# Pinned splits and earlier loads of late operands, tile 19 by token halves, and a shorter sum for one product in a hybrid attention and MLP trunk

## The chip, the core and the metric

The kernel runs on one core of a Trainium2 chip. A core has a matrix engine (PE), three engines for elementwise work (DVE, ACT, POOL), a queue that issues transfers (SP; POOL issues some too) and 16 DMA engines that carry them. Every engine works through its own queue in order, and semaphores hold an instruction back until what it reads or overwrites is ready. Matrix products are accumulated in PSUM, eight banks of 128x512 numbers; all else on the core lies in SBUF.

The metric is the device time of one execution in microseconds (us). The kernel before took a median of 1145.42 us in three runs (1144.83 to 1148.57).

## The reference

One layer of a streaming encoder with 1024 tokens and a model width of 1024, all in 32-bit floats:

```python
hn = rmsnorm(h, norm_mix_g);  z = hn @ w_in              # 1024 -> 512 pooling + 3 x 512 attention
a  = pool_mixer(u);  o = chunk_attention(q, k, v, rel_bias)
h  = h + concat([a, o]) @ w_out
hn = rmsnorm(h, norm_ffn_g);  up = hn @ w_up             # 1024 -> 2 x 2816
gt, val = up[..., :2816], up[..., 2816:]
gt = causal_dwconv(gt, conv_w, conv_b)                   # width 3 over tokens
h  = h + (gelu(gt) * val) @ w_down                       # 2816 -> 1024
hn = rmsnorm(h, norm_ple_g);  gate = sigmoid(hn @ w_ple_gate + b_ple_gate)
h  = h + gate * (p @ w_ple)
out = rmsnorm(h, final_g)
```

The change lies in the gated MLP (`w_up`, the convolution, `w_down`) and in the operands of the last stage (`w_ple`, `p`).

## The kernel before

**Numbers in two parts.** PE takes a rounded form of a 32-bit float, so each operand is cut into a rounded part and a remainder. `split` does that with two instructions: ACT copies the source into the rounded part (L133), then DVE subtracts that from the source (L134). A product is three matmuls (`mm3`, L128 to L130): high by high, high by low, low by high.

**Stages.** Attention and pooling mixer with the input projection run to about 275 us, the output projection to about 380 us, the MLP from there to about 998 us, and the projection of `p`, the gate and the final norm to the end.

**The up-projection.** The 2816 hidden features are 22 tiles (`NF`) of 128, numbered from 0. For each tile, the weights form a 2x2 block matrix (gate and value rows by two halves of the width) and the activations another (two halves of the width by two halves of the tokens, `HS`). A form of fast matrix multiplication takes seven products in place of eight; they carry the numbers 1 to 7, and `FORMS` says which weight blocks each one sums. A product is four `mm3` into one PSUM bank, 12 matmuls. `steps` holds the order of a tile's products: (1, 5, 6, 2, 7, 3, 4), except for tiles 0 and 1, parts of which are done ahead (`ahead`). For tile 1 the order is (5, 6, 2, 7, 3, 4). Below, (21, 6) is product 6 of tile 21.

For each product `prepare` loads the weight blocks it still needs from `w_up` into one of six raw buffers (`rawu`, SP, L695), sums them in place on DVE (`summed`, L699) and splits the sum into one of three weight buffers (`wu`). It does that three products ahead, and `fetch` asks for loads three further products ahead.

`step` then runs the product and moves its result on. `keep` copies a bank to SBUF on ACT (L784), `seed` copies one bank into another with a sign (L788), and the DVE lines 807 to 821 finish gate and value. A product that adds into a bank whose earlier content is still to be copied away has to wait for that copy. `gate` does the convolution and GELU: ACT (L833), DVE twice (L834, L835), ACT (L836). For tiles in `halved` it runs by token halves, otherwise once over 1024 tokens.

**The down-projection.** Tiles 0 to 19 go to `w_down` in five groups (0 to 4) of four tiles, by the same kind of fast multiplication: seven products per group in `DOWN_ORDER` (1, 2, 5, 4, 6, 7, 3), each of 24 matmuls into banks 4 to 7 (`down_next`). Their places between the up products are fixed (`places`, `downs`). A finished tile is written to device memory (`Yd`, SP, L891); `ask` loads blocks of it and of `w_down` into eight raw buffers (`RW`): one pair "one" and one pair "grow" for each side, weights `w` and activations `a`. The first block of a sum is a plain load by SP (L942), each further block is a load by POOL that adds to what is there (L940). `DOWN_W` and `DOWN_A` list the blocks. On the activation side product 4 sums four blocks, so each of its two buffers takes one plain load and three adding ones; product 6 adds one more block to product 5's sum in "grow". `split_next` splits the four buffers into `BQ` and `R`: w, w, a, a, with L133 and L134, or with L972 and L973 where the activation's sign is turned (products 2, 4, 7). Each split of a product waits until the product before has read the pair, so it falls between two down products. Below, (4,4) in "down (4,4)" is product 4 of group 4.

Tiles 20 and 21 are kept on the core (`store`, buffers `gv2`) and multiplied directly later (`down_mm`).

**Late operands.** The raw weights of tiles 20 and 21 (`w_down`), `w_ple` and `p` are loaded through `late_pair` into `rawu` buffers that have come free (SP, L1041) and split into `wd2`, `wp` and `pt`: twelve pieces of 256 KB. Six are written after products 2 and 3 of tile 21, six after that tile.

**What sets the order.** PE runs its instructions in the order of the program. For the other engines and for SP a planner chooses when the program is built: among the instructions that it takes to be ready at a moment of its own timetable it takes the one that stands first in the program, and those under `tc.high_priority(AHEAD)` are treated as if they stood 60 instructions earlier. So an instruction can come long before its place in the program. In the queue that results the order is then fixed, and an instruction whose data comes later than the timetable had it holds up all behind it.

## Time and profile before

| what | value |
|---|---|
| median of three runs | 1145.42 us |
| profiled execution, its own time | 1146.88 us |
| its span, first to last instruction | 1145.1 us |
| mean granted clock of PE | 0.995 |
| PE busy | 1129.9 us, 99%, 5675 matmuls |
| DVE busy | 888.2 us, 78% |
| ACT busy | 604.7 us, 53% |
| POOL busy | 146.8 us, 13% |
| moved by DMA | 125.89 MB, 110 GB/s |

A page of the profile gives for each engine its busy time, then the span in 40 slices, then the chain of waits and the costliest groups of instructions. A timeline row holds start, duration, engine, line, operation, tiles, shape, how many instructions it stands for, and in brackets how long the engine had been idle before it and what ended that. A row of stretches holds, for one stretch of the span, its length, the busy time of each engine with its number of instructions, the granted clock of PE, the share of the DMA engines in use and GB/s.

### The profile page before, as it was taken

Reading aid. Unit: us, or ns where it says so; the run is one execution under the profiler, and the core shown is the slowest. Engines: PE = TensorE matmul, PEld = TensorE weight load, DVE = VectorE, ACT = ScalarE, POOL = GpSimd, SP = SyncE. Lnnn points to the kernel's source line nnn. Section 1 sums busy time; section 2 is a strip of 40 time slices with the busy share of each in tenths; the row PEclk is TensorE's granted clock in tenths of the full one; section 3 lists DMA queues with packets and bytes.
Section 4 is the critical chain, followed back from the end, with each engine's and each line's share of the span. In section 5 each row is a group of like instructions: output and inputs, shape, how many; then the busy total and the mean of one; then the engine's idle time right before and its main releaser. Section 6 shows DMA issues by size and latency. Waiting matters only on the chain.

```text
span 1145.1 us, 15750 instructions
## 1 busy us (share of the span) xinstructions
PE 1129.9 (99%) x5675; PEld 958.2 (84%) x5675; DVE 888.2 (78%) x1541; ACT 604.7 (53%) x1068; POOL 146.8 (13%) x192
## 2 busy tenths in 40 slices
PE   9999999999999999999999999999999999999997
PEld 7988998888888778888888888888888887788897
DVE  7678878879658787888787878777887788986864
ACT  8568677765554554444444444443444344664644
POOL 0000000073002200120112011201120113000000
PEclk9999999999999999999999999999999999999999
DMA  7110101104500343575557655755575559320012
GB/s 265 37 49 31 50 12 68 40 28 151 172 19 10 97 128 117 140 172 140 144 144 162 158 148 146 173 141 145 152 172 138 145 148 183 114 92 19 1 74 74
DMA packets 65022, 125.89 MB, mean 110 GB/s; under 512 B 7344, under 2 KB 8624, under 8 KB 64944
## 3 DMA queue, kind: packets, MB, share of 16 engines
q1 hardware_dynamic: 50400, 98.60, 25.9%
q0 software_dynamic: 14400, 26.22, 14.1%
q8 instruction: 44, 0.72, 0.3%
q14 instruction: 34, 0.28, 0.1%
q10 hardware_dynamic: 144, 0.07, 0.0%
HBM read 110.18 MB, written 14.68 MB: 109 GB/s over the span
## 4 chain that ended last, share of the span: by engine, by line
PE 93%; issue 2%; ACT 2%; DMA 1%; DVE 1%; SPq 0%; POOL 0%; POOLq 0%; DVEq 0%; ACTq 0%
PE PS L128 28%; PE PS L129 28%; PE PS L130 28%; PE PS L367 2%; PE PS L385 1%; PE PS L384 1%; DMA F<-in_w_down 1%; PE PS L342 1%; PE PS L341 1%; DMA F<-in_w_qk 0%; PE PS L350 0%; PE PS L349 0%; PE PS L617 0%; DMA RW<-in_w_down 0%; ACT F L353 0%
## 5 line engine op out<-in xcount | busy, mean ns | idle before, releaser
L128 PE MATMUL PS<-R 128*128 128x512 f32 (+1 forms) x1176 | 443.2, 377 | 2.8 <-ACT F L784 2.1
L130 PE MATMUL PS<-R 128*128 128x512 f32 (+1 forms) x1176 | 438.4, 373 | 0.0
L129 PE MATMUL PS<-R 128*128 128x512 f32 (+1 forms) x1112 | 420.8, 378 | 0.3 <-DVE R L230 0.3
L128 PEld LDWEIGHTS PS<-R 128*128 128x128 f32 x1176 | 222.1, 189 | 40.7 <-ACT F L784 2.8
L130 PEld LDWEIGHTS PS<-R 128*128 128x128 f32 x1176 | 222.1, 189 | 39.1
L129 PEld LDWEIGHTS PS<-R 128*128 128x128 f32 x1112 | 210.0, 189 | 37.1 <-DVE R L230 0.9
L133 ACT ACTIVATE R<-F 128x512 fp32r<-128x512 f32 (+2 forms) x225 | 141.3, 637 | 186.1 <-PE PS L129 76.4
L134 DVE TENSOR_TENSOR R<-F,R 128x512 fp32r<-128x512 f32 (+2 forms) x221 | 152.8, 699 | 53.2 <-ACT R L133 52.3
L133 ACT ACTIVATE BQ<-RW 128x512 fp32r<-128x512 f32 x90 | 52.8, 623 | 85.5 <-PE PS L129 78.8
L990 DVE TENSOR_TENSOR F<-F,PS 128x512 f32<-128x512 f32 x140 | 92.3, 680 | 4.4 <-PE PS L130 4.3
L699 DVE TENSOR_TENSOR F<-F 128x512 f32<-128x512 f32 x88 | 60.5, 687 | 44.1 <-DMA F<-in_w_up 41.0
L940 POOL DMA_DIRECT2D RW<-Yd x60 | 52.4, 873 | 267.2 <-DMA RW<-Yd 215.2
L940 POOL DMA_DIRECT2D RW<-in_w_down x40 | 36.1, 951 | 227.1 <-DMA RW<-in_w_down 190.1
L134 DVE TENSOR_TENSOR BQ<-RW,BQ 128x512 fp32r<-128x512 f32 x90 | 59.1, 684 | 5.6 <-ACT BQ L133 4.3
L129 PE MATMUL PS<-BQ 128*128 128x512 f32 x140 | 54.9, 392 | 2.7 <-DVE BQ L973 2.7
L353 ACT ACTIVATE F<-F,small 128x640 f32<-128x640 f32 (+2 forms) x64 | 44.4, 693 | 21.1 <-DVE small L351 13.1
L128 PE MATMUL PS<-BQ 128*128 128x512 f32 x140 | 54.8, 392 | 0.3 <-ACT BQ L972 0.3
L128 PE MATMUL PS<-R,BQ 128*128 128x512 f32 x140 | 55.0, 393 | 0.0
L129 PE MATMUL PS<-R,BQ 128*128 128x512 f32 x140 | 54.9, 392 | 0.0
L130 PE MATMUL PS<-BQ 128*128 128x512 f32 x140 | 54.8, 391 | 0.0
L130 PE MATMUL PS<-R,BQ 128*128 128x512 f32 x140 | 54.7, 391 | 0.0
L609 ACT ACTIVATE F<-F 128x512 f32<-128x512 f32 (+1 forms) x49 | 27.9, 569 | 44.6 <-DVE F L1145 16.7
(186 smaller groups left out, 1803.0 us busy)
## 6 DMA issues: line engine op xcount, KB each, us to landing
F<-in_w_up SPq DMA_DIRECT2D x91, 256.0 KB, 4.2
RW<-Yd SPq DMA_DIRECT2D x60, 256.0 KB, 3.7
RW<-Yd POOLq DMA_DIRECT2D x60, 256.0 KB, 5.1
RW<-in_w_down SPq DMA_DIRECT2D x50, 256.0 KB, 2.8
RW<-in_w_down POOLq DMA_DIRECT2D x40, 256.0 KB, 6.2
Yd<-F SPq DMA_DIRECT2D x40, 256.0 KB, 2.4
F<-in_w_in SPq DMA_DIRECT2D x10, 512.0 KB, 3.5
F<-in_xT SPq DMA_DIRECT2D x16, 256.0 KB, 5.8
```

Of the source, the lines that this page charges most:

```text
L128: pe.matmul(ps, ahi, bhi, start=first, stop=False, skip_group_check=more)
L129: pe.matmul(ps, ahi, blo, start=False, stop=False, skip_group_check=more)
L130: pe.matmul(ps, alo, bhi, start=False, stop=last, skip_group_check=more)
L133: act.activation(hi, src, AF.Copy)
L134: dve.tensor_tensor(lo, src, rv(hi), ALU.subtract)
L341: pe.matmul(PS[:, 4 + z, 0:320], q, K2[:, ks], start=True, stop=False)
L353: act.activation(S[:, 0:n], S[:, 0:n], AF.Exp, bias=s_[:, 0:1], scale=-1.0, accum_out=s_[:, 1:2])
L367: pe.transpose(pst[:, j * P:(j + 1) * P], S[:, j * P:(j + 1) * P], ident)
L609: act.activation(self.q, src, AF.Square)
L699: dve.tensor_tensor(rawu[to], rawu[a], rawu[b], op)
L940: pool.dma_start(t, src, accum_op=ALU.add)
L990: dve.tensor_tensor(t, t, PS[:, 4 + d], ALU.subtract if n in (1, 5) else ALU.add)
```

## The change

It has eight parts.

- `split` takes `pinned`. A pinned instruction may not be put ahead of the instruction that stands before it in the program on its engine (`tc.keep_in_program_order`); those that stand after it are still free to overtake it.
- The loads of the first group's first blocks (`ask(True)`, after tile 1) and the first split of the down-projection (`split_next(True)`, after tile 2) are pinned.
- A GELU of one column is put behind the splits of the output weights; it is pinned.
- `fetch` asks six products ahead in place of three for the first seven.
- Tile 1's products come in the order (5, 2, 6, 3, 7, 4). Its weight sums go as tile 0's do, and its product 4 starts in a fresh bank and adds a kept copy of product 7, where it had started in a bank seeded from it.
- Tile 19 (`NF - 3`) is treated by token halves: convolution and GELU, value, store and the request for what depends on it.
- Down (4,4) on the activation side: per buffer one plain load and one adding load, and DVE adds the sum of product 5 that stands in "grow". The adding loads of down (4,6) into "grow" then wait for that.
- The twelve late pieces come in a new order (`w_down`, half of `p`, `w_ple`, the other half), through all six buffers, pinned, behind products 5, 6, 7 and 4 of tile 21: two, four, four and two.

```diff
--- before.py
+++ after.py
...
-        def split(src, hi, lo):
-            act.activation(hi, src, AF.Copy)
-            dve.tensor_tensor(lo, src, rv(hi), ALU.subtract)
+        def split(src, hi, lo, pinned=False):
+            both = (act.activation(hi, src, AF.Copy),
+                    dve.tensor_tensor(lo, src, rv(hi), ALU.subtract))
+            if pinned:
+                for i in both:
+                    tc.keep_in_program_order(i)
...
         out_weights(0, pooled)
+        tc.keep_in_program_order(act.activation(small[:, 2:3], mhalf, AF.Gelu))
         norm_a = Norm(HS[0], tmp[0], tmp[2:3], 6, 6)
...
         alone = ahead[:3]
-        steps = {0: (6, 3, 7, 4), 1: (5, 6, 2, 7, 3, 4)}
+        steps = {0: (6, 3, 7, 4), 1: (5, 2, 6, 3, 7, 4)}
         for fi in range(2, NF):
...
                 prepared[0] += 1
-                fetch(prepared[0] + 3)
+                fetch(prepared[0] + (3 if prepared[0] > 7 else 6))
                 assert fetched[0] == len(loads) or loads[fetched[0]][0] >= prepared[0]
...
                         summed(a21, a21, a11)
-                    elif n == 3 and not fi:
+                    elif n == 3 and fi < 2:
                         summed(a11, a21, a12)
                     elif n == 7:
-                        if fi:
+                        if fi > 1:
                             summed(a11, a21, a12)
...
                     t = {1: a11, 5: a21, 2: a12, 6: a21, 3: a11, 7: a21, 4: a22}[n]
-                    done_with = {3: [a11, a12], 7: [a21], 4: [a22]}.get(n, []) if fi == 0 else {
+                    done_with = {3: [a11, a12], 7: [a21], 4: [a22]}.get(n, []) if fi < 2 else {
                         3: [a11], 7: [a12, a21], 4: [a22]}.get(n, [])
...
         firsts = {0: (0, 3, 5, 4), 1: (2, 3, 1, 5)}
-        halved = (1, NF - 1)
+        halved = (1, NF - 3, NF - 1)
...
             x, y, z, w = firsts.get(fi, (0, 1, 2, 3))
-            product({1: x, 2: x, 5: z, 3: z, 6: y, 7: y, 4: w}[n], n in (1, 5) or (fi, n) == (0, 4))
+            product({1: x, 2: x, 5: z, 3: z, 6: y, 7: y, 4: w}[n], n in (1, 5) or n == 4 and fi < 2)
             if n == 1 and fi != 1:
...
             elif n == 7:
-                if fi:
+                if fi > 1:
                     seed(w, y)
...
             elif n == 4:
-                if fi:
+                if fi > 1:
                     dve.tensor_tensor(V[:, HS[0]], PS[:, w], rst[:, HS[0]], ALU.mult)
...
             for h in range(2):
+                if HS[h].stop <= ts.start or HS[h].start >= ts.stop:
+                    continue
                 y = Yb[:, HS[h]]
...
-                values_in(slice(0, SEQ), dst)
-                for ts in HS:
-                    sp.dma_start(Yd[fi][:, ts], Yb[:, ts])
-                stored.add(fi)
-                ask()
+                for part in [HS[0:1], HS[1:2]] if fi == NF - 3 else [HS]:
+                    values_in(slice(part[0].start, part[-1].stop), dst)
+                    for ts in part:
+                        sp.dma_start(Yd[fi][:, ts], Yb[:, ts])
+                        stored.add((fi, HS.index(ts)))
+                    ask()
                 if fi > 3:
...
+        def parts(side, g, n):
+
+            if (side, g, n) == ("a", 4, 4):
+                return DOWN_A[4][::3], False
+            own, growing = (DOWN_W, GROWING_W) if side == "w" else (DOWN_A, GROWING_A)
+            return own[n], n in growing[1:]
+
         def sources(side, g, n):
...
                 if side == "w":
-                    yield j, [w_down[group_of(g)[2 * k + j], :, i * 512:(i + 1) * 512] for i, k in DOWN_W[n]]
+                    yield j, [w_down[group_of(g)[2 * k + j], :, i * 512:(i + 1) * 512] for i, k in parts(side, g, n)[0]]
                 else:
-                    yield j, [Yd[group_of(g)[2 * k + j]][:, HS[t]] for k, t in DOWN_A[n]]
+                    yield j, [Yd[group_of(g)[2 * k + j]][:, HS[t]] for k, t in parts(side, g, n)[0]]
...
-        def ask():
+        def ask(pinned=False):
...
                             break
-                        if side == "a" and not all(group_of(g)[2 * k + j] in stored for k, _ in DOWN_A[n] for j in range(2)):
+                        if side == "a" and not all((group_of(g)[2 * k + j], t) in stored for k, t in parts(side, g, n)[0] for j in range(2)):
                             break
...
                         asked.add((side, g, n))
-                        grown = n in (GROWING_W if side == "w" else GROWING_A)[1:]
+                        grown = parts(side, g, n)[1]
                         for j, srcs in sources(side, g, n):
...
                                 else:
-                                    sp.dma_start(t, src)
+                                    i = sp.dma_start(t, src)
+                                    if pinned:
+                                        tc.keep_in_program_order(i)
...
                         if buffer(side, n) == kind:
-                            queue.append((g, n, before))
+                            queue.append((g, n, (4, 4) if (side, g, n) == ("a", 4, 6) else before))
                             before = (g, n)
...
-        def split_next():
+        def split_next(pinned=False):
             if nsplit[0] == len(sequence) or nsplit[0] > ndown[0]:
...
                     hi, lo = pairs[side, j]
+                    if (side, g, n) == ("a", 4, 4):
+                        dve.tensor_tensor(t, t, raws["a", "grow", j], ALU.add)
                     if sign > 0:
-                        split(t, hi, lo)
+                        split(t, hi, lo, pinned)
                     else:
...
                             raws[side, kind, j] = RW[:, 512 * z:512 * (z + 1)]
-                ask()
+                ask(True)
             if fi == 2:
...
                 ask()
-                split_next()
+                split_next(True)
         places = [(1, 5), (2, 6), (3,), (0, 4)]
...
         nl = len(loads)
-        late = [rawu[(nl + z) % 6] for z in (0, 1)]
-        nlate = [0]
-
-        def late_pair(src, hi, lo):
-            t = late[nlate[0] % len(late)]
-            nlate[0] += 1
-            sp.dma_start(t, src)
-            split(t, hi, lo)
-
-        def ple_weights():
-            for k in range(2):
-                for z in HS:
-                    late_pair(w_ple[k, :, z], wp[k][0][:, z], wp[k][1][:, z])
-
-        def ple_rows(h):
-            for k in range(2):
-                late_pair(pT[k, :, HS[h]], *pt[h][k])
-
-        def down_weights(fi, dst):
-            for z in HS:
-                late_pair(w_down[fi, :, z], dst[0][:, z], dst[1][:, z])
+        late = [rawu[(nl + z) % 6] for z in (0, 1, 5, 3, 2, 0, 1, 5, 3, 4, 2, 0)]
+        pieces = []
+        for z, fi in enumerate(last_f):
+            pieces += [(w_down[fi, :, ts], wd2[z][0][:, ts], wd2[z][1][:, ts]) for ts in HS]
+        pieces += [(pT[k, :, HS[0]], *pt[0][k]) for k in range(2)]
+        for k in range(2):
+            pieces += [(w_ple[k, :, ts], wp[k][0][:, ts], wp[k][1][:, ts]) for ts in HS]
+        pieces += [(pT[k, :, HS[1]], *pt[1][k]) for k in range(2)]
+        npiece = [0]
+
+        def late_pairs(n):
+            for _ in range(n):
+                src, hi, lo = pieces[npiece[0]]
+                t = late[npiece[0]]
+                npiece[0] += 1
+                sp.dma_start(t, src)
+                split(t, hi, lo, True)
...
         hooks = downs(last_f[1], (0, 2, 4, 6))
-        for n, fn in ((1, lambda: store(gv2[0])), (2, ple_weights), (3, lambda: ple_rows(0)),
-                      (4, lambda: late.extend(rawu[(nl + z) % 6] for z in (2, 3, 4, 5)))):
-            hooks.setdefault(n, []).insert(0, fn)
+        hooks.setdefault(1, []).insert(0, lambda: store(gv2[0]))
+        for n, many in ((5, 2), (6, 4), (7, 4), (4, 2)):
+            hooks.setdefault(n, []).insert(0, lambda many=many: late_pairs(many))
         up(last_f[1], gv2[1], hooks)
...
-        down_weights(last_f[0], wd2[0])
-        down_weights(last_f[1], wd2[1])
-        ple_rows(1)
         for d in range(KT):
...

```

## The prediction, made before the changed kernel was run

> **What bounds the kernel now.** I read the page first (PE busy in every slice), then the list of what PE waited for, then PE's timeline around each wait, then the queues of ACT and DVE at the same moments, and at the end the stretches. First two stretches, which give PE's pace and its clock.
>
> ```profile
> 396.44:400.00 3.56, 3.56 (x9) 2.78 (x10) 3.33 (x6) 2.01 (x4) 1.98 (x2) 0.53 0.85 281
> ...
> 420.00:954.00 534.00, 534.00 (x2357) 442.19 (x2356) 426.49 (x651) 233.36 (x375) 79.58 (x91) 1.00 0.59 148
> ...
> 980.20:983.80 3.60, 3.60 (x10) 2.79 (x9) 3.60 (x7) 1.39 (x3) 0.00 (x0) 0.53 0.31 98
> ```
>
> From 420 to 954 PE never idles: 534.00 us for 2357 matmuls, 0.2266 each. No matmul is added or removed by the change, so all that can be won is where PE falls off this pace. Between tile 0 and the end of the MLP there are four such places in PE's timeline:
>
> ```profile
> 390.90 0.50 PE L128 MATMUL PS<-R 128*128 128x512 f32 x1
> ...
> 393.76 0.60 PE L625 MATMUL PS<-ident,small 128*128 128x128 f32 x4
> 396.44 0.63 PE L128 MATMUL PS<-R 128*128 128x512 f32 x1 [2.08 <-ACT F L784]
> ...
> 400.88 0.39 PE L128 MATMUL PS<-R 128*128 128x512 f32 x1
> ...
> 406.10 0.39 PE L130 MATMUL PS<-R 128*128 128x512 f32 x1
> 407.17 0.50 PE L128 MATMUL PS<-R 128*128 128x512 f32 x1 [0.68 <-ACT PS L788]
> ...
> 410.04 0.39 PE L128 MATMUL PS<-R 128*128 128x512 f32 x1
> ...
> 954.04 0.39 PE L128 MATMUL PS<-BQ 128*128 128x512 f32 x1
> 955.55 0.50 PE L129 MATMUL PS<-BQ 128*128 128x512 f32 x1 [1.13 <-DVE BQ L973]
> ...
> 960.93 0.39 PE L128 MATMUL PS<-R 128*128 128x512 f32 x1
> ...
> 977.03 0.39 PE L130 MATMUL PS<-R 128*128 128x512 f32 x1
> 977.74 0.49 PE L128 MATMUL PS<-BQ 128*128 128x512 f32 x1 [0.33 <-ACT BQ L972]
> 979.83 0.50 PE L129 MATMUL PS<-BQ 128*128 128x512 f32 x1 [1.59 <-DVE BQ L973]
> ...
> 986.80 0.39 PE L128 MATMUL PS<-R 128*128 128x512 f32 x1
> ```
>
> - Wait A, before (0,7). From 390.90 to 400.88 there are two products and four transposes: 24 x 0.2266 = 5.44, and 0.44 for the transposes (four of this line at another place, quoted below), 5.88 in all. It took 9.98, so A costs 4.10.
> - Wait B, before tile 1's product 6. From 406.10 to 410.04, 13 matmuls are worth 2.95; 3.94 - 2.95 = 0.99.
> - Wait C, in down (4,4). From 954.04 to 960.93, 24 matmuls are worth 5.44; 6.89 - 5.44 = 1.45.
> - Wait D, in down (4,7). From 977.03 to 986.80, 25 matmuls are worth 5.67; 9.77 - 5.67 = 4.10.
>
> Together 10.64. In A and D part of this is not idle time: behind them the granted clock is 0.53, and 9 and 10 matmuls run where 3.56 / 0.2266 = 15.7 and 3.60 / 0.2266 = 15.9 would, which costs 6.7 x 0.2266 = 1.52 and 5.9 x 0.2266 = 1.33. Idle gaps of 2.08 (A) and of 0.33 and 1.59 close together (D) brought the slow clock; those of 0.68 (B) and 1.13 (C) did not.
>
> **The change part by part.** For A and B, the queue of ACT, with one row of the chain of waits and one of DVE:
>
> ```profile
> 342.30 0.44 PE PS L625 x4
> ...
> 390.27 0.58 ACT L784 ACTIVATE F<-PS 128x512 f32<-128x512 f32 x1
> 394.75 0.63 ACT L133 ACTIVATE BQ<-RW 128x512 fp32r<-128x512 f32 x1 [3.90 <-DMA RW<-in_w_down]
> ...
> 395.81 0.58 ACT L784 ACTIVATE F<-PS 128x512 f32<-128x512 f32 x1
> ...
> 403.74 0.68 DVE L815 TENSOR_TENSOR V<-PS,F 128x512 f32<-128x512 f32 x1
> ...
> 404.28 1.28 ACT L836 ACT_TABLE_LOAD   x1
> ...
> 406.54 0.58 ACT L788 ACTIVATE PS<-PS 128x512 f32<-128x512 f32 x1
> ```
>
> *A.* ACT stood 3.90 before a split of `w_down` for the first down product, which PE needs only after tile 3. The `keep` that PE was waiting for (L784 at 395.81) had been ready since (0,6) ended, about 391, but stood behind it. Pinning sends this split behind tile 2. Then the `keep` runs at about 391, before the transposes are through. Late next is the weight split of (0,4); it stands between the rows of 394.75 and 395.81 and moves forward with the queue, and PE wants it at 394.2 + 2.72 = 396.9. I take A as gone, -4.10; ends 0 and -4.10. What is moved: eight `w_down` loads of SP and two of POOL and two splits (ACT about 1.2, DVE about 1.4) go to where the stretch from 420 shows DVE at 426.49 of 534 and ACT at 233.36. On SP the loads now stand behind tile 1's stores. `w_up` loads may be held up behind them, but `prepare` runs three products (3 x 2.72 us) ahead. I take 0.
>
> *B.* The `seed` (L788) came right behind a table load of 1.28 and a GELU. It needs DVE's L815 (ended at 404.42). Without the table load it would run from about 405.3 to 405.9, before PE needs it at 406.33. The new order puts product 2 in product 6's place, but product 2 adds to the very bank that the seed reads, so the deadline stays. With A gone PE comes 4.1 earlier; DVE, whose half of the same splits goes too, gains about 1.4 and what it waited behind ACT, up to 3.9. I take B as gone, -0.99, ends 0 and -0.99. The extra addition for tile 1 (0.68) and the earlier loads are covered by the same slack; I take 0 of 0 to 0.7.
>
> *The early GELU* moves the 1.28 load and a tiny GELU to 312.18 - 9.28 = 302.9, where ACT idles (quoted below). Cost 0.
>
> For C and D, with the durations from issue to landing of POOL's adding loads (930 to 970) and of the late loads, in this order:
>
> ```profile
> 312.18 0.63 ACT L607 ACTIVATE F<-F 128x512 f32<-128x512 f32 x1 [9.28 <-DVE F L646]
> ...
> 952.08 0.63 ACT L972 ACTIVATE R<-RW 128x512 fp32r<-128x512 f32 x1 [2.46 <-DMA RW<-Yd]
> ...
> 954.21 0.69 DVE L134 TENSOR_TENSOR R<-F,R 128x512 fp32r<-128x512 f32 x1 [1.00 <-ACT R L133]
> 954.82 0.68 DVE L973 SCALAR_TENSOR_TENSOR BQ<-RW,BQ 128x512 fp32r<-128x512 f32 x1
> ...
> 967.02 1.10 SPq L1041 DMA_DIRECT2D F<-in_w_down  x2
> ...
> 967.42 0.62 ACT L133 ACTIVATE R<-F 128x512 fp32r<-128x512 f32 x1
> 974.16 0.63 ACT L133 ACTIVATE R<-F 128x512 fp32r<-128x512 f32 x1 [6.12 <-DMA F<-in_w_down]
> 976.01 0.63 ACT L133 ACTIVATE R<-F 128x512 fp32r<-128x512 f32 x1 [1.22 <-DMA F<-in_w_down]
> 976.55 0.62 ACT L133 ACTIVATE BQ<-RW 128x512 fp32r<-128x512 f32 x1
> ...
> DMA to landing us min/median/max: 3.7/5.2/8.0
> ...
> DMA to landing us min/median/max: 2.5/2.9/8.2
> ```
>
> And the stretches of the last two tiles (busy times in the order PE, weight loads, DVE, ACT, POOL):
>
> ```profile
> 900.00:921.00 21.00, 21.00 (x95) 17.38 (x94) 14.87 (x24) 7.40 (x13) 2.80 (x4) 1.00 0.57 136
> ...
> 943.00:954.00 11.00, 11.00 (x50) 9.13 (x49) 10.17 (x15) 5.48 (x8) 5.24 (x6) 1.00 0.87 139
> 954.00:966.00 12.00, 10.87 (x48) 8.63 (x48) 11.39 (x17) 5.40 (x10) 3.51 (x4) 1.00 0.86 193
> 966.00:978.00 12.00, 11.67 (x52) 9.31 (x50) 5.97 (x10) 4.52 (x9) 1.74 (x2) 1.00 0.75 163
> 978.00:998.00 20.00, 18.41 (x74) 14.84 (x74) 20.00 (x33) 12.02 (x22) 0.00 (x0) 0.91 0.37 119
> ```
>
> *C.* The activation blocks of down (4,4) landed at 952 as the last of six adding loads in POOL's queue. ACT waited 2.46, DVE behind it, and the low part that PE needed came at 954.82. The three adding loads into one buffer go one behind the other; two of three fall away, so at the median of 5.2 the last lands by 952 - 10.4 = 941.6, and tile 19's earlier store helps. In their place DVE gets two additions (0.68 each, by the like row) where it is busy 10.17 of 11.00. So the load is no longer late, but DVE may be: of the 1.36 I put 0.6 on PE. C gives -0.85; ends -1.45 and -0.1. The halves of tile 19 add at most two DVE passes of about 0.7, where DVE has 21.00 - 14.87 = 6.1 free: 0. The adding loads for (4,6) now wait for the two additions; these can run from 942 on, and PE wants (4,6) at 960.93 + 5.44 = 966.4: at 8.0 us a load, 0.
>
> *D.* ACT stood 6.12 and 1.22 before two late splits of `w_down`, and the splits of down (4,7) from 976.55 stood behind them. Their loads left at 967.02, when the buffers came free, and took the 7 to 8 us of the maximum. In the new order the first three of the six pieces behind products 5 and 6 have their buffers early. The fourth reuses the buffer that was freed at 967.02, the fifth that of (21,3), whose split is the row of 967.42, so about 969; the sixth comes between. The splits of (4,7) can start when (4,6) has been read, at 966.4 + 5.44 = 971.8, and must start by about 974.5 (PE wants the third of four at 977.26; they start 0.54 apart, and DVE's part follows 0.7 behind). With the median 2.9 the fifth lands at 972 and nothing waits, -4.10. With the maximum 8.2 it lands at 977, and the wait is about 2 longer than now, +2. The DMA engines carry less there than before: four adding loads are gone, and those of (4,7) leave earlier, as (4,4) is split earlier. I take 5 us: landing 974.2, two splits to 975.3, a wait of about 1 without the slow clock. D gives -3.1; ends +2 and -4.1.
>
> *The rest of the twelve pieces.* Their number is unchanged; DVE does up to six of them (6 x 0.68 = 4.1) sooner than before. It is full from 978 on, but the 6.03 that it stands in 966 to 978 is free once ACT isn't held. I take 0; ends 0 and +4.1.
>
> **Sum.** -4.10 - 0.99 - 0.85 - 3.1 = -9.0. The profiled execution has a span of 1145.1 and a time of its own of 1146.88, 1.46 above the median of 1145.42. The gains are differences inside it, taken from the median: 1136.4. All four whole: 1145.42 - 10.64 = 1134.8.
>
> The slow clock is 2.85 of this sum. The Trainium skill, "TensorE: Matmul & The Clock Gate" (Why this matters for your kernels), asks for "No PE-idle gaps >~3µs between matmul bursts", by which gaps of 1.9 and 2.08 would be harmless and the slow clock be due to something else. The trace disagrees: it has the clock at 0.53 behind just these two.
>
> **The rivals.**
>
> 1. *D stays.* ACT's order again has the fourth and fifth late split ahead of (4,7), and their loads take 7 to 8 us. For it: in the present trace the planner put such splits there; DMA is busy 0.86 of 954 to 966. Against: the lower DMA load. Only A, B and 0.85 of C: 1145.42 - 5.94 = 1139.5. Chance 0.18.
> 2. *The wait at tile 0 only moves.* With A gone, PE meets the next late thing, the seed or a weight split: DVE at 403.74 was only 0.6 ahead of need. Then C and D alone, 1145.42 - 3.95 = 1141.5. Against it: ACT is freed of 3.90 and 1.28 there. Chance 0.13.
> 3. *The slow clock is not tied to the waits* and comes anyway: 1136.4 + 2.85 = 1139.3. Against it are the two gaps of C and B without it. Chance 0.04. It is the rule of the page of the Trainium skill named above that would have it so.
> 4. *Slower: DVE becomes the bound of tile 21.* Pinned pieces keep ACT waiting as before, so the free 6.03 is lost again, and DVE must do twelve remainders and two additions, 14 x 0.68 = 9.5, ahead of what PE needs before 998, with two more stretches of slow clock (2.9). That puts up to 12.4 on PE against A's and B's 5.09: 1152.7. It decides once more than 5.09 + 3.44 = 8.5 lands on PE. For it: 20.00 of 20.00. Against: much of this work is already done there today, and PE needs `gv2` and the rest only after the projection of `p`. Chance 0.15.
>
> **How the numbers follow.** My forecast has 0.50, by itself 1134.8 to 1138.5. About 0.3%, or 3.44 us, is what can be told from no change: 1141.98 and 1148.86. Faster: 0.50 + 0.18 + 0.04 and half of rival 2, 0.78; the same: the other half, 0.07; slower: 0.15. The range goes from 1134.5 (all four waits gone) past rivals 1 to 3 to 1143.0; rival 4 and a part of 2 lie outside.
>
> **What would show it.** A: no row of ACT waiting for `w_down` near 394, and (0,7) right behind the transposes. B: the GELU table load at about 303, and no wait on L788. C: POOL's last load for (4,4) landed by 942, and the row of L973 before its matmul. D: no ACT wait for a late load between 967 and 977. Clock 1.00 throughout from 380 to 1050. The prediction is wrong if PE shows new waits in 395 to 410 or between 950 and 1010, above all on DVE.

## The result and the profile after

The changed kernel took 1149.33 us (median of 22 runs, 1145.45 to 1151.89), the kernel before 1145.95 in the same comparison (22 runs, 1144.00 to 1148.57). The ratio is 1.0026, 95% interval 1.0016 to 1.0035: a little slower, where the prediction had 1136.4.

The profiled execution of the changed kernel is the shortest of its 22 runs (1145.45, span 1143.7), so the losses shown here are at the low end. Between 380 and 1000 PE runs at its pace (0.2266 us per matmul) except at three places that count. Rows of PE's timeline after the change:

```profile
402.34 0.39 PE L130 MATMUL PS<-R 128*128 128x512 f32 x1
404.94 0.50 PE L128 MATMUL PS<-R 128*128 128x512 f32 x1 [2.20 <-ACT PS L792]
405.27 0.40 PE L129 MATMUL PS<-R 128*128 128x512 f32 x1
...
940.94 0.39 PE L128 MATMUL PS<-BQ 128*128 128x512 f32 x1
943.31 0.50 PE L129 MATMUL PS<-BQ 128*128 128x512 f32 x1 [1.98 <-DVE BQ L134]
...
950.25 0.39 PE L128 MATMUL PS<-R 128*128 128x512 f32 x1
...
977.23 0.39 PE L130 MATMUL PS<-R 128*128 128x512 f32 x1
977.84 0.50 PE L128 MATMUL PS<-BQ 128*128 128x512 f32 x1 [0.23 <-ACT BQ L990]
979.49 0.50 PE L129 MATMUL PS<-BQ 128*128 128x512 f32 x1 [1.14 <-DVE BQ L991]
...
985.37 0.39 PE L128 MATMUL PS<-R 128*128 128x512 f32 x1
```

Counted as in the prediction: before tile 1's product 2, two matmuls in 402.34 to 405.27, 2.93 - 0.45 = 2.48; in down (4,5), 24 matmuls in 940.94 to 950.25, 9.31 - 5.44 = 3.87; before and in down (4,7), 25 in 977.23 to 985.37, 8.14 - 5.67 = 2.47. Together 8.8, where the kernel before had 10.64. Waits A and C of the prediction are gone, B has grown and moved, D is smaller in this execution, and the largest loss, in (4,5), stands where the kernel before had none. Two stretches show the same, and the clock (busy times in the order PE, weight loads, DVE, ACT, POOL, then granted clock):

```profile
402.00:410.00 8.00, 5.80 (x26) 4.47 (x25) 7.82 (x13) 3.21 (x5) 0.00 (x0) 1.00 0.49 144
...
940.00:948.00 8.00, 6.02 (x20) 4.46 (x19) 7.96 (x14) 1.01 (x2) 3.52 (x4) 0.79 0.56 85
```

**At tile 1.** First SP, then DVE, then ACT, and the landing times of the `w_up` loads between 390 and 400:

```profile
391.07 0.80 SPq L956 DMA_DIRECT2D RW<-in_w_down  x2
...
392.60 0.90 SPq L956 DMA_DIRECT2D RW<-in_w_down  x2
393.60 0.38 SPq L699 DMA_DIRECT2D F<-in_w_up  x1
...
398.90 1.42 DVE L703 TENSOR_TENSOR F<-F 128x512 f32<-128x512 f32 x2 [2.80 <-DMA F<-in_w_up]
...
403.34 1.06 ACT L840 ACTIVATE F<-F 128x1024 f32<-128x1024 f32 x1 [2.84 <-DVE F L839]
404.30 0.58 ACT L792 ACTIVATE PS<-PS 128x512 f32<-128x512 f32 x1
...
DMA to landing us min/median/max: 2.6/4.6/5.2
```

The four plain `w_down` loads still leave at 391.07 and 392.60, ahead of tile 1's stores. The `w_up` load of 393.60, right behind them, is the one that took 5.2. DVE stood 2.80 for it; behind it stand L838 and L839 of the gate, behind these on ACT the GELU and then the seed that PE waits for.

**In down (4,5).** POOL's queue, DVE's queue and POOL's landing times:

```profile
931.41 0.86 POOL L954 DMA_DIRECT2D RW<-Yd  x1 [28.09 <-DMA RW<-Yd]
933.40 0.86 POOL L954 DMA_DIRECT2D RW<-Yd  x1 [1.12 <-issue]
...
935.97 0.69 DVE L986 TENSOR_TENSOR RW<-RW 128x512 f32<-128x512 f32 x1 [5.61 <-DMA RW<-Yd]
...
941.97 1.28 DVE L134 TENSOR_TENSOR BQ<-RW,BQ 128x512 fp32r<-128x512 f32 x2
...
DMA to landing us min/median/max: 4.5/4.6/4.7
```

L986 is the first of DVE's two additions for (4,4). The planner put it before the remainders of (4,5). It stood 5.61 for a load that landed at about 931.41 + 4.5, and work piled up behind it; the remainder that PE needs is the second of the row at 941.97 and ended at 943.25.

**Before (4,7).** ACT, and the landing times of the late pieces issued between 966 and 970:

```profile
973.85 0.63 ACT L133 ACTIVATE R<-F 128x512 fp32r<-128x512 f32 x1 [5.60 <-DMA F<-in_w_down]
975.07 1.15 ACT L133 ACTIVATE R<-F 128x512 fp32r<-128x512 f32 x2 [0.60 <-DMA F<-in_pT]
976.13 1.14 ACT L133 ACTIVATE BQ<-RW 128x512 fp32r<-128x512 f32 x2
...
DMA to landing us min/median/max: 6.7/6.9/6.9
```

Now three late pieces stand ahead of the splits of (4,7), where two did before.

Over the 22 runs the mean granted clock is 0.995, against 0.997 over the runs of the kernel before; 0.002 of 1147 is 2.3 us, an estimate of what a slow clock behind more of these gaps adds in a usual run.

### The profile page after: what moved, and what is told of

The parts are those of the page before. It is cut to its first block, busy times and chain, and to the rows that moved or that the text cites. A ratio compares the mean times of both kernels' runs of the same rounds, so it can differ in the third digit from the quotient of the medians.

```text
span 1143.7 us, 15749 instructions
## 1 busy us (share of the span) xinstructions
PE 1127.9 (99%) x5675; PEld 956.1 (84%) x5675; DVE 889.5 (78%) x1546; ACT 604.6 (53%) x1071; POOL 142.9 (12%) x188
## 4 chain that ended last, share of the span: by engine, by line
PE 88%; DVE 4%; issue 2%; ACT 2%; DMA 1%; POOL 1%; SPq 0%; DVEq 0%; POOLq 0%; ACTq 0%
PE PS L129 27%; PE PS L128 27%; PE PS L130 27%; PE PS L370 2%; DVE R L134 2%; PE PS L388 1%; PE PS L387 1%; PE PS L345 1%; PE PS L344 1%; ACT R L133 1%; DMA F<-in_w_down 1%; DMA F<-in_w_up 0%; DMA F<-in_w_qk 0%; PE PS L353 0%; PE PS L352 0%
## 5 line engine op out<-in xcount | busy, mean ns | idle before, releaser
L954 POOL DMA_DIRECT2D RW<-Yd x56 | 49.0, 876 | 256.4 <-DMA RW<-Yd 209.1
L837 ACT ACTIVATE F<-F,vec 128x1024 f32<-128x1024 f32 (+1 forms) x25 | 28.6, 1143 | 53.4 <-DVE F L812 49.7
```

What stands on the lines that cost most here:

```text
L837: act.activation(y, Gb[:, 2 + a:2 + b], AF.Identity, bias=vec[:, C_CB + fi:C_CB + fi + 1], scale=cw(2))
L954: pool.dma_start(t, src, accum_op=ALU.add)
```

## The experiments

The theory after the first look was that the losses at (4,5) and before (4,7) cancel the gains at tile 0, and that the addition in (4,4) is the main one. The rival was the late pieces. Line numbers differ by a few between the kernels; the operation is named each time.

**after_again**: the changed kernel once more.

> The changed kernel as it is, one further profiled execution. The first profile (1145.45 us) was the shortest of 22 runs whose median is 1149.33, so it shows too little. If the waits that depend on the landing of transfers vary from run to run (theory 1), this execution has the same places of PE waiting (before tile 1's product 2, in down (4,5), in down (4,7)) with 2 to 5 us more in them and a clock of 0.993 to 0.995. If the extra time comes from another place (rival), new waits of PE stand in the list that the first profile has not.

Measured: 1147.54, one run, 2.09 more than the first profile. The three places are the same; here the clock is low twice, behind the gap in (4,5) and behind that in (4,7):

```profile
943.80:947.30 3.50, 3.50 (x10) 2.68 (x10) 3.47 (x7) 0.00 (x0) 2.11 (x3) 0.51 0.92 133
981.30:984.90 3.60, 3.60 (x9) 2.79 (x10) 2.72 (x5) 3.16 (x6) 0.00 (x0) 0.53 0.25 73
```

So (4,7) loses 4.3 here against 2.47, which is most of the 2.09. This run still lies 1.8 below the median of the changed kernel, and no profile shows where a usual run loses those.

**no_c44**: product (4,4) as before, with six adding loads and no addition on DVE.

```diff
-            if (side, g, n) == ("a", 4, 4):
-                return DOWN_A[4][::3], False
...
-                    if (side, g, n) == ("a", 4, 4):
-                        dve.tensor_tensor(t, t, raws["a", "grow", j], ALU.add)
```

> The changed kernel with down (4,4) loaded as before (one plain and three adding loads per buffer, no addition on DVE); all else as changed. Theory 1, the addition on DVE, which stands in DVE's queue ahead of work for down (4,5) and waits for a load, costs 3.9 us in (4,5) and more in most runs: then the wait in (4,5) is gone, wait C (1.45) is back, and the time falls by 2.5 to 6 us from 1149.3, to 1143.3 to 1146.8. Rival, the late splits in tile 21 make the kernel slower: no change, 1149 within 1.

Measured: 1151.03 (9 runs), ratio to before 1.0046 (1.0030 to 1.0061). The wait in (4,5) went, and a larger one came in (4,4). PE's row there:

```profile
956.71 0.80 PE L129 MATMUL PS<-BQ 128*128 128x512 f32 x1 [4.51 <-DVE BQ L987]
```

So my theory, that taking the addition out makes the kernel faster, fell. By the medians the shorter sum takes 1.7 off the changed kernel, but the two intervals overlap. What the addition costs in one place it saves in another. This run keeps the halves of tile 19, and the 4.51 has a cause of its own, which halves_alone shows below.

**no_late**: the twelve late pieces as before (`late_pair`, two raw buffers, not pinned), all else as changed.

```diff
-        for n, many in ((5, 2), (6, 4), (7, 4), (4, 2)):
-            hooks.setdefault(n, []).insert(0, lambda many=many: late_pairs(many))
+        for n, fn in ((1, lambda: store(gv2[0])), (2, ple_weights), (3, lambda: ple_rows(0)),
...
+        down_weights(last_f[0], wd2[0])
```

> The changed kernel with the twelve late pieces as before (two buffers first, six pieces behind tile 21, not pinned). Theory 1: the late pieces are not what makes it slower; wait D goes back from about 2.2 to 4.1, and the time is 1149.3 to 1152. Rival, the late splits cost: the time falls by 3 us or more, below 1146.3.

Measured: 1146.52 (11 runs), ratio 1.0008 (0.9995 to 1.0020), 2.8 below the changed kernel. That is close to the 3 which the rival asked for and far from theory 1: the new late pieces cost. The wait at (4,5) stays, as it should.

**start_only**: only the parts at the start (pins, early GELU, earlier fetch, tile 1's order); tile 19, (4,4) and the late pieces as before.

```diff
-        halved = (1, NF - 3, NF - 1)
+        halved = (1, NF - 1)
...
-                for part in [HS[0:1], HS[1:2]] if fi == NF - 3 else [HS]:
+                for part in [HS]:
```

> Only the parts at the start of the MLP (pinned first split and its loads, early GELU, loads six ahead, tile 1's order); tile 19, down (4,4) and the late pieces as before. Theory 1: wait A is gone (-4.1), wait B grows from 1.0 to 2.4 (+1.4): 1145.95 - 2.7 = 1143.2. Rival, the wait at the start only moves in the typical run: 1145.9 within 1.

Measured: 1143.62 (11 runs), ratio 0.9985 (0.9972 to 0.9999), against 1145.86 of the kernel before; near theory 1. So by the medians the start gives -2.2, tile 19 with the shorter sum +2.9 (no_late against start_only), the late pieces +2.8 (the changed kernel against no_late). In the profile PE has no gap in (4,4), and one of 0.85 in (4,7), which loses 1.1 in all:

```profile
977.17 0.50 PE L129 MATMUL PS<-BQ 128*128 128x512 f32 x1 [0.85 <-DVE BQ L987]
```

Both products are treated here as in the kernel before, where they lost 1.45 and 4.10. So these two waits are not of a fixed size that the change could take off.

From here the theory was one of order: each part puts an instruction that waits for a transfer in front of one that PE needs, in a queue that is worked through in order.

**later_loads**: start_only, with the first `w_down` loads pinned behind tile 2's stores.

```diff
-                ask(True)
+                pass
...
-                    ask()
+                    ask(fi == 2)
```

> The kernel start_only, with the first w_down loads of the first group really behind a store on SP: they leave after tile 2's stores, and no w_down load stands among tile 0's and tile 1's w_up loads. Start_only had a median of 1143.6, and at 402 PE lost 4.1 in its profile (2.0 to 4.5 in the four other profiles that have the new start). Theory 1 (the w_up load that tile 1's sum waits for took 5.2 us instead of some 2.5 because the w_down loads left beside it): the wait of 2.8 of DVE's sum and the wait of PE for tile 1's seed go, 1140.0 to 1141.5. Theory 2 (the sum and the GELU are late because of tile 1's new order, product 2 in front of product 6): the loss at 402 stays, 1143 to 1144.

Measured: 1142.37 (12 runs), ratio 0.9970 (0.9959 to 0.9981). The `w_up` loads between 390 and 394 now land in 2.6 to 2.8 (the last of them left at 393.2, so it is the landing that changed, not the issue), DVE's sum comes 2.5 earlier than in the changed kernel and waits for nothing, and PE has no gap from 396 to 410:

```profile
396.41 1.41 DVE L703 TENSOR_TENSOR F<-F 128x512 f32<-128x512 f32 x2
...
DMA to landing us min/median/max: 2.6/2.7/2.8
...
396.00:410.00 14.00, 14.00 (x64) 11.58 (x63) 12.48 (x19) 7.95 (x12) 0.00 (x0) 1.00 0.30 95
```

That shows the cause of the loss at 402: the loads beside it. Tile 1's new order alone brings no wait. The median fell by 1.2, less than the 2.1 to 3.6 expected, and the two intervals overlap. The profiled execution (1145.51, one of the longest) shows other losses in place of this one: 6.2 in (4,7), where ACT stood 7.76 for the late pieces and the clock went down, and 1.1 each in (4,4) and near 459. PE's row in (4,7):

```profile
977.28 0.79 PE L129 MATMUL PS<-BQ 128*128 128x512 f32 x1 [2.27 <-DVE BQ L987]
```

**pinned_add**: no_late, with the two additions kept in program order, beside the splits of (4,4).

```diff
-                        dve.tensor_tensor(t, t, raws["a", "grow", j], ALU.add)
+                        tc.keep_in_program_order(dve.tensor_tensor(t, t, raws["a", "grow", j], ALU.add))
```

> The kernel no_late, with DVE's two additions for down (4,4) kept in program order, so that they stand beside the splits of (4,4) and no longer 24 instructions ahead of them, in front of the splits of (4,5). No_late had a median of 1146.5 and its profile lost 5.9 on PE at 944. Theory 1 (an addition placed early holds DVE's whole queue until POOL's loads have landed): the loss at 944 goes, about 1142. Theory 2 (DVE has too much to do between 943 and 954, where it was busy 10.17 of 11.00, and the order does not matter): the loss moves to (4,4) at 951 to 956, 1145 to 1147.

Measured: 1148.53 (11 runs), ratio 1.0019 (1.0008 to 1.0030). The wait in (4,5) is gone, but (4,4) waits again and again, and the granted clock is 0.50 from 957.0 to 963.5. Two of PE's rows there:

```profile
953.69 0.51 PE L128 MATMUL PS<-BQ 128*128 128x512 f32 x1 [1.00 <-ACT BQ L990]
...
956.70 0.79 PE L128 MATMUL PS<-R,BQ 128*128 128x512 f32 x1 [1.13 <-ACT R L990]
```

The time lies above both ranges; by the place of the loss this speaks for theory 2, that the additions are too much for DVE. But they now stood on the chain of (4,4) itself: addition, rounded part, remainder. So a third place was tried.

**mid_add**: no_late, with the additions right behind the splits of (4,5).

```diff
-                    if (side, g, n) == ("a", 4, 4):
-                        dve.tensor_tensor(t, t, raws["a", "grow", j], ALU.add)
...
+            if (g, n) == (4, 5):
+                for j in range(2):
+                    t = raws["a", "one", j]
+                    tc.keep_in_program_order(dve.tensor_tensor(t, t, raws["a", "grow", j], ALU.add))
```

> The kernel no_late (1146.5), with DVE's two additions for (4,4) put right behind the splits of (4,5) and kept there: neither ahead of the splits of (4,5), where they held the queue, nor beside the splits of (4,4), where they came late in pinned_add. Theory 1 (the additions cost by their place in DVE's queue): no wait of PE at 940 to 944 and none at 952 to 958, 1141.0 to 1142.7, that is start_only's 1143.6 less up to 1.1 and some spread. Theory 2 (the two additions, 1.4 of DVE, are too much for it there, wherever they stand): a loss of 3 or more between 940 and 965, 1145 to 1148.

Measured: 1144.36 (12 runs), ratio 0.9988 (0.9975 to 1.0002). Neither range was hit: 2.2 better than no_late, where 3.8 or more was expected. Both additions run without a wait, and (4,5) has no loss; one wait of 1.33 is left in (4,4). DVE has no pause from 935.8 to 956 here, so its amount of work may have a share in that wait; but all_moved, with the same additions in the same place, has none there. The first addition on DVE, and PE's row:

```profile
941.19 0.68 DVE L995 TENSOR_TENSOR RW<-RW 128x512 f32<-128x512 f32 x1
...
954.06 0.50 PE L129 MATMUL PS<-BQ 128*128 128x512 f32 x1 [1.33 <-DVE BQ L989]
```

**halves_alone**: start_only and tile 19 by token halves, nothing else.

```diff
-        halved = (1, NF - 1)
+        halved = (1, NF - 3, NF - 1)
...
-                for part in [HS]:
+                for part in [HS[0:1], HS[1:2]] if fi == NF - 3 else [HS]:
```

> The kernel start_only with tile 19's values by halves and its two stores apart, and nothing else. Theory 1 (the additions in (4,4) bring the loss, by their place in DVE's queue; the halves cost at most two DVE passes of 0.7): 1143.0 to 1144.3. Theory 2 (the halves bring the 2.9 by which no_late stands above start_only, by another order of loads and splits around (4,5) and (4,4)): 1146 to 1147.

Measured: 1147.92 (10 runs, 1145.14 to 1154.37), ratio 1.0020 (1.0002 to 1.0038). The halves, which I had put at nothing, cost 4.3. POOL's queue and the ACT row it leads to:

```profile
931.29 0.86 POOL L952 DMA_DIRECT2D RW<-Yd  x1 [27.71 <-DMA RW<-Yd]
937.83 1.78 POOL L952 DMA_DIRECT2D RW<-Yd  x2 [5.67 <-DMA F<-in_w_ple]
941.88 0.87 POOL L952 DMA_DIRECT2D RW<-Yd  x1 [2.27 <-DMA RW<-Yd]
943.97 0.86 POOL L952 DMA_DIRECT2D RW<-Yd  x1 [1.22 <-DMA RW<-Yd]
948.40 0.86 POOL L952 DMA_DIRECT2D RW<-Yd  x1 [3.57 <-DMA RW<-Yd]
...
952.83 0.63 ACT L986 ACTIVATE R<-RW 128x512 fp32r<-128x512 f32 x1 [4.99 <-DMA RW<-Yd]
```

These are the six adding loads of (4,4), three for each of two buffers. With the new store times the planner put the first buffer's first two behind each other. The second had to wait until the first landed, and the other buffer's first, whose plain load was already in place, stood behind it: it is the second of the pair at 937.83. (The row names a `w_ple` load as what ended the wait; it landed 0.2 after the adding load.)

**halves_pool**: halves_alone, with the six loads kept in turn between the two buffers.

```diff
+                        if (side, g, n) == ("a", 4, 4):
+                            turns = [(j, z, both[j][1][z]) for z in range(4) for j in range(2)]
...
+                                    if (side, g, n) == ("a", 4, 4):
+                                        tc.keep_in_program_order(i)
```

> The kernel halves_alone (1147.9), with the six adding loads of (4,4) kept in turn between the two buffers on POOL, as in start_only; in halves_alone two for one buffer followed each other, the second waited for the first to land, and the first for the other buffer stood behind it from 934 to 938. Theory 1 (the halves cost by this order alone): the last adding load lands about 2 to 3 us earlier, by 950.5, the loss of 3.9 at 952 goes, 1142.8 to 1144.3. Theory 2 (it is DVE's and ACT's order around the halves): 1146 to 1148.

Measured: 1144.50 (12 runs), ratio 0.9984 (0.9970 to 0.9997); 3.4 better than halves_alone and within the noise of start_only. POOL's second and last adding loads, and the same split on ACT:

```profile
935.61 0.86 POOL L956 DMA_DIRECT2D RW<-Yd  x1 [1.77 <-issue]
...
945.86 0.86 POOL L956 DMA_DIRECT2D RW<-Yd  x1 [1.60 <-issue]
...
950.30 0.63 ACT L992 ACTIVATE R<-RW 128x512 fp32r<-128x512 f32 x1 [0.16 <-DMA RW<-Yd]
```

The last load leaves 2.5 earlier although the first left 1.7 later. The order in POOL's queue was the cost of the halves.

**late_alone**: start_only and the late pieces in the new places.

```diff
+        for n, many in ((5, 2), (6, 4), (7, 4), (4, 2)):
+            hooks.setdefault(n, []).insert(0, lambda many=many: late_pairs(many))
```

> The kernel start_only with the twelve late pieces in the new places, and nothing else of tile 19 and (4,4). Theory 1 (the late pieces cost by themselves, since ACT waits for them ahead of the splits of (4,7)): start_only's 1143.6 and the 2.8 by which after stands above no_late, 1146.4. Theory 2 (they cost only in company with the new (4,4), whose splits and loads they meet): the small loss of 1.1 at 976 goes, 1142.5 to 1143.6.

Measured: 1146.66 (10 runs), ratio 0.9999 (0.9989 to 1.0010): 3.0 above start_only. The late pieces cost by themselves: (4,7) loses 4.7 in the profile, against 1.1 in start_only. On ACT its splits come behind them:

```profile
975.96 1.13 ACT L133 ACTIVATE BQ<-RW 128x512 fp32r<-128x512 f32 x2
```

**late_behind**: late_alone, with the four pieces after product 6 behind the down product of that place, and so behind the splits of (4,7).

```diff
-            hooks.setdefault(n, []).insert(0, lambda many=many: late_pairs(many))
+            hooks.setdefault(n, []).insert(1 if n == 6 else 0, lambda many=many: late_pairs(many))
```

> The kernel late_alone (1146.7), with the four late pieces of product 6 behind the down product of the same place and so behind the splits of (4,7), and no longer ahead of them. Theory 1 (ACT stands before the late pieces, whose loads take 6.7 to 8.0 us, and the splits of (4,7) stand behind it): the loss of 4.6 at 976 goes, 1142.0 to 1143.6. Theory 2 (the splits of (4,7) wait for their own loads, which leave at the same time and take as long): the loss stays, 1146 to 1147.

Measured: 1142.87 (12 runs), ratio 0.9968 (0.9955 to 0.9980), 3.8 better. On ACT the splits of (4,7) come at 971.18, 4.8 earlier, and the late pieces wait behind them:

```profile
971.18 0.63 ACT L133 ACTIVATE BQ<-RW 128x512 fp32r<-128x512 f32 x1 [3.63 <-issue]
...
974.82 0.63 ACT L133 ACTIVATE R<-F 128x512 fp32r<-128x512 f32 x1 [0.93 <-DMA F<-in_w_down]
```

**all_moved**: the changed kernel with the edits of later_loads, mid_add and late_behind together.

```diff
-                ask(True)
+                pass
...
-                    ask()
+                    ask(fi == 2)
...
+            if (g, n) == (4, 5):
+                for j in range(2):
...
+            hooks.setdefault(n, []).insert(1 if n == 6 else 0, lambda many=many: late_pairs(many))
```

> The changed kernel with all its parts, and three of them moved: the w_down loads behind tile 2's stores (later_loads), the additions for (4,4) behind the splits of (4,5) (mid_add), the four late pieces behind the splits of (4,7) (late_behind). Theory 1 (it was only the places in the queues): nothing left of the losses at 402, 944 and 977, so 1149.3 less 2.0 to 4.5, 3.8 and 2.4 to 4.3, and what the spread of the slow clock adds: 1137 to 1140. Theory 2 (with each wait that goes, the next late thing comes up): 1141 to 1144.

Measured: 1139.08 (6 runs, 1137.91 to 1141.12), ratio 0.9937 (0.9921 to 0.9954): faster than both kernels, 6.7 below the 1145.77 of the kernel before in that comparison and 10.2 below the changed one. The stretch from 380 to 1000, first of the kernel before, then of this one:

```profile
380.00:1000.00 620.00, 614.14 (x2699) 506.64 (x2698) 496.29 (x761) 278.63 (x451) 91.52 (x102) 0.99 0.58 148
```

```profile
380.00:1000.00 620.00, 619.05 (x2739) 511.94 (x2738) 507.16 (x781) 283.66 (x460) 87.89 (x98) 1.00 0.58 148
```

It has all eight parts of the change, and as many instructions on PE, DVE, ACT and POOL as the changed kernel. What differs is where three groups of instructions stand. One wait is left between 380 and 1000, a new one; later_loads has it too (0.82 at 458.81), so it came with the moved `w_down` loads (PE's row):

```profile
459.30 0.50 PE L130 MATMUL PS<-R 128*128 128x512 f32 x1 [0.90 <-DVE R L134]
```

The gains of the mended parts do not add up. Against start_only's 1143.62, later_loads has -1.2, mid_add +0.7 and late_behind -0.7; all together have -4.5. Part of this is the uncertainty of each median (the intervals are some 1.5 us wide to each side). Whether a wait left standing also uses up what a mended one gave was not settled; the profile of later_loads, with its 6.2 in (4,7), looks like it, but it is one execution.

## Why the prediction was wrong, point by point

The prediction took four waits out of one profile and subtracted them. What failed was the order in the queues: in four steps it took an instruction to stand in another place, or to cost only its own duration there.

- **A gone, -4.10**: right. From 396 PE runs at its pace up to 402.34, and no row of ACT waits for `w_down` near 394. The parts of the start were not run one by one; by the medians they gave 2.2 together.
- **B gone, -0.99 ("the deadline stays")**: wrong. It grew to 2.48 in the profile. The step that failed is "On SP the loads now stand behind tile 1's stores": they left at 391.07 to 392.60. A pin holds an instruction only behind the one before it in the program on its queue, and before the first of these loads that is the marker which opens their buffer pool, as the built program lists it, and not a store. The sentence that `prepare` runs three products ahead, so that `w_up` loads could be held up for nothing, failed with it: DVE was free for tile 1's sum 2.5 after the issue of its load, and the load took 5.2. In later_loads the `w_down` loads do leave behind stores, and both the late load and the wait are gone.
- **The early GELU, 0**: right; the table load is at about 301 and cost nothing.
- **C, -0.85**: the load came early, even earlier than worked out (about 936 and 938 against 942), and the wait in (4,4) went. But the 0.6 for the two additions was mis-sized. It priced them as 1.36 of work on a busy engine, not by their place: ahead of the remainders of (4,5), one of them held DVE for 5.61, and PE lost 3.87 in a product that the prediction did not look at. The forecast's own picture, that they "can run from 942 on", describes mid_add (941.19). The wait in (4,4) is also gone in start_only, which has none of this part, so its 1.45 can't be credited to the shorter sum.
- **The halves of tile 19, 0**: wrong by 4.3 taken alone. DVE's free time did cover the passes; what was left out is that earlier stores let the planner order POOL's loads anew (halves_pool). With the shorter sum POOL has only two such loads, so this cost can't come on top of that of the addition: together +2.9.
- **D, -3.1**: wrong. The late pieces cost 2.8 to 3.0 by the medians, more than the upper end of +2. The loads took 6.7 to 6.9 where I had taken 5, and three pieces stood before the splits of (4,7), one more than before. late_behind shows that the place decides. The 4.10 to be won was mis-sized too: with the late pieces as before, the profiles lost 4.10 (before), 1.1 (start_only) and 6.2 (later_loads) in (4,7).
- **The sum**, taken from one profiled execution with two stretches at low clock and 1.46 above the median, was also too large: the runs of the kernel before have a mean clock of 0.997, that execution 0.995. all_moved, which has the four waits gone and one new one, gained 6.7, not 9 or more.
- **The rivals.** Rival 2 ("the wait at tile 0 only moves", 0.13) named the seed, and it was the seed: of A and B's 5.09 the start kept 2.2. Rival 1 ("D stays", 0.18) held too in what it says of ACT's order and of the loads. Rival 4, slower, got its beginning right (pinned pieces keep ACT waiting) but not its price; nothing like 12 landed on PE. The slower outcome came from several of these at once, and from (4,5), which no rival had. The range ended at 1143.0, below the result.
- **Clock 1.00 throughout** did not hold: 0.79 from 940 to 948.

## What to carry to other kernels

Price an added or moved instruction by what stands behind it in its queue while it waits, not by its own duration: here 1.36 us of additions, in three places of DVE's queue, made a difference of 4 us (pinned_add against mid_add). When a planner sets the order, an edit that changes when something becomes ready (an earlier store, a pin) can reorder queues that the edit does not mention, so list each queue of the built program, POOL's and SP's among them, before and after. A pin is worth only what stands before it: look up which instruction that is. And a wait read from one profile is not yet a saving: look at it in a second execution before subtracting it.

## What the runs showed of the hardware that was not expected

**Gaps and the slow clock.** A gap of 1.98 in (4,5) was followed by the low clock (0.79 from 940 to 948 above). One of 2.20 before tile 1's product 2 was not, though 2.22 at the same place in start_only was. And one of 3.65 in halves_alone was not. Rows of start_only:

```profile
405.69 0.50 PE L128 MATMUL PS<-R 128*128 128x512 f32 x1 [2.22 <-ACT PS L792]
...
406.40:410.00 3.60, 3.60 (x11) 2.78 (x10) 3.07 (x6) 0.27 (x1) 0.00 (x0) 0.53 0.31 98
```

Rows of halves_alone:

```profile
956.31 0.50 PE L129 MATMUL PS<-BQ 128*128 128x512 f32 x1 [3.65 <-DVE BQ L987]
...
956.30:960.00 3.70, 3.69 (x16) 3.05 (x17) 3.70 (x6) 0.17 (x1) 2.62 (x3) 1.00 1.07 215
```

Before tile 1's product 2 eleven profiles have a gap: those of 2.05 (halves_pool), 2.22, 2.35 (late_behind) and 2.65 (no_late) were followed by the low clock, and those of 1.67 to 1.94, 2.09 (no_c44), 2.20 and 2.37 (late_alone) were not. So the length of a gap does not decide it alone, and the prediction's reading of A and D, that these gaps bring it and those of B and C do not, rested on too few cases. The Trainium skill, "TensorE: Matmul & The Clock Gate" (Part 1, What's actually happening), has the clock set by activity in a window of about 3.4 us that runs freely; that the phase of such a window decides would fit these rows, but no run here shows the window.

**Transfers.** A load of 256 KB took 2.6 to 2.8 with at most its own neighbours in the `w_up` series beside it (later_loads), 5.2 right behind the four `w_down` loads (the changed kernel at 393.60) and 6.7 to 6.9 for the late pieces, which left close together behind two plain loads of `Yd` and among POOL's adding loads; no run separates these. The Trainium skill, "DMA: Bandwidth & Descriptors" (Anatomy of one DMA), fits POOL's loads by 2.0 us and the bytes at 436 GB/s, which makes 2.6 for this size, an estimate. The adding loads in (4,5) took 4.5 to 4.7; it is the plain load of later_loads, issued by SP, that comes to the page's figure.
